# Gaps of 32 bytes between the pairs of transposed input tiles in SBUF

## The chip, the cores and the metric

The kernel runs on one core of a Trainium2 chip. The metric is the device time of one execution in microseconds (us). Two runs of the kernel before took 3258.87 and 3260.27 us, median 3259.57 us.

## The reference

Three transformer layers on one sequence of 512 tokens, width 1024, all in float32. Two layers have the form: half a gated feed-forward block (1024 to 2816 and back), a mixer of three branches (differential attention, chunked attention with a relative bias, retention) that are gated and summed, and another half feed-forward block. The third layer has dilated attention, a state-space scan and a gated linear recurrence side by side, then a feed-forward block and a final norm. Cut to what matters here, nearly all work is a matrix product of a normalised input with a weight matrix:

```
h = rms_norm(x, norm)
x = x + 0.5 * ((silu(h @ w_gate) * (h @ w_up)) @ w_down)
...
aq, ak, av, bq, bk, bv, cq, ck, cv, cg, gates = split(rms_norm(x, mix_norm) @ w_in)
```

## The kernel before, in words

The input is kept transposed: 8 tiles of 128 features by 512 tokens. A product of float32 precision is made of three single-pass matmuls in the type float32r. Each operand is split into a high part and a low part, and `mm3` (lines 406 to 411) issues high by high, low by high and high by low, into one accumulator in PSUM. This triple is the unit in which the prediction counts:

```
self.matmul(out, st[0], mv[0], start, False, c)
self.matmul(out, st[0], mv[1], False, False, c)
self.matmul(out, st[1], mv[0], False, stop, c)
```

`st` is the stationary operand, which is loaded into the array ahead of its matmul (the trace calls the load LDWEIGHTS, engine PEld), and `mv` the moving one, which streams through. In the trace a name out<-in,in gives the moving operand first.

The tiles in question are the 8 pairs `xgh0,xgl0` to `xgh7,xgl7`: high and low part of the scaled input, 128 partitions by 512 float32 each, 2048 bytes in a partition. `feed_norm` (line 591) allocates and fills them, one pair for each of the 8 blocks d of the features. They are used in two ways. In `fm_tile` (line 637) they are the moving operand and a weight block is stationary: 8 triples with d = 0 to 7, 512 columns each, make one output tile. In `tm_products` (line 644) the roles change: a slice of 128 tokens of `xgh` or `xgl` is stationary and the weights move, 384 or 512 columns. The weights are read from DRAM into the ring `raw` and split by ScalarE and VectorE into the rings `wh` and `wl` (lines 503 to 513), three buffers each, 4096 bytes in a partition; a unit of weights holds 8 blocks of 128 columns, 512 bytes each.

Tiles of one pool lie one behind the other in the order in which their names are first used, each rounded up to 32 bytes. Call the address of a tile within the partition, modulo 256, its place. In the kernel before, `wh` and `wl` start at 34048 and 46336, all 16 tiles `xgh`, `xgl` from 75008 on, 2048 bytes apart, and the feed-forward tiles `yh`, `yl` from 133888 and 156416 on: all these are at place 0, and so is every block of 512 bytes within them. A tile `warm` of 57 floats (line 452) ends the constants such that the rings behind it start at place 0.

One small unit of weights is different. `dt_unit` (line 1802) holds 8 blocks of only 8 columns each, 32 bytes, for a product with 8 outputs in the third layer. So its stationary operands lie at the places 0, 32, 64 and so on to 224, while the moving `xgh` and `xgl` are at 0. In the trace its matmuls are `b<-xgh,wh 128*8`.

The order of the program is made when it is built: a list scheduler with a cost for each operation resumes threads (`Net.ready`, `Net.wait`, class `Model`). Its numbers of buffers are those of the pools. The small tiles of the norm and the softmax (`rsy`, `rst`: 64 bytes, 7 buffers each; `nmax`, `sm`, `rc`: 32 bytes, 8 buffers each) lie in the pool behind the inputs.

## Time and profile before

| | |
|---|---|
| median of 2 runs | 3259.57 us |
| profiled execution, its own time | 3257.48 us |
| its span, first to last instruction | 3255.7 us |
| PE busy | 3232.1 us, 99% of the span, 15592 matmuls |
| PEld (weight loads) busy | 2713.4 us, 83% |
| DVE (VectorE) busy | 1870.9 us, 57% |
| ACT (ScalarE) busy | 1233.6 us, 38% |
| DMA, mean rate | 106 GB/s |
| mean granted TensorE clock | 0.996 of full speed |

1.8 us of the profiled execution's time lie around its span. A matmul is shown as busy from its start until its result is out, so consecutive matmuls overlap in the trace: one of 512 columns is shown as 389 ns long, and the next one starts well before its end. What a matmul takes from the engine is therefore read from start to start, called a step below, and not from its duration.

### The profile page before, as it was taken

What the parts mean: (1) busy time and instruction counts of PE and PEld (TensorE: products, weight loads), DVE (VectorE), ACT (ScalarE), POOL (GpSimd) and SP (SyncE); (2) the same over time, 40 slices, a digit from 0 to 9 for tenths busy, and PEclk for the clock granted to TensorE, in tenths of its full rate; (3) what the DMA queues carried; (4) which work ended last, traced back from release to release, by engine and by line L of the source; (5) the groups of instructions that cost most, each with busy time, mean ns of one, the idle gap of its engine ahead of it and who ended that gap; (6) DMA issues with size and microseconds to landing.
All of it is one profiled execution on the core that took longest, in us unless ns stands there. A gap on an engine that the chain in (4) does not pass through costs nothing.

```text
span 3255.7 us, 39837 instructions
## 1 busy us (share of the span) xinstructions
PE 3232.1 (99%) x15592; PEld 2713.4 (83%) x15592; DVE 1870.9 (57%) x3574; ACT 1233.6 (38%) x1996; POOL 111.6 (3%) x206
## 2 busy tenths in 40 slices
PE   9999999999999999999999999999999999999998
PEld 7888888878888888888888987888888788888888
DVE  5434578766754345434478766664344777564345
ACT  4223344653332223322344564333223346643223
POOL 0000000000100000000010000110000000000000
PEclk9999999999999999999999999999999999999999
DMA  4222443223423222222243322442223223222224
GB/s 143 97 97 97 130 118 112 88 84 110 171 92 102 95 94 97 97 97 97 94 138 115 112 90 76 139 149 97 97 97 110 103 72 106 81 88 97 97 97 143
DMA packets 106413, 343.51 MB, mean 106 GB/s; under 512 B 19680, under 2 KB 20864, under 8 KB 106224
## 3 DMA queue, kind: packets, MB, share of 16 engines
q1 hardware_dynamic: 83520, 289.04, 26.2%
q0 software_dynamic: 22704, 51.93, 4.6%
q8 instruction: 122, 2.00, 0.3%
q14 instruction: 67, 0.55, 0.1%
HBM read 319.88 MB, written 26.21 MB: 106 GB/s over the span
## 4 chain that ended last, share of the span: by engine, by line
PE 98%; DVE 1%; DMA 0%; ACT 0%; issue 0%; SPq 0%; DVEq 0%
PE acc L404 90%; PE b L404 7%; PE b L433 2%; DMA raw<-in_wst_dram 0%; DMA rowsA<-in_rows_dram 0%; DVE o L203 0%; DVE og L203 0%; ACT v L203 0%; DVE v L203 0%; DVE pT L203 0%; DVE y L203 0%; SPq L224 0%; DVE rst L203 0%; ACT y L203 0%; ACT pT L203 0%
## 5 line engine op out<-in xcount | busy, mean ns | idle before, releaser
L404 PE MATMUL acc<-xgh,wh 128*128 128x512 f32 x2432 | 959.4, 394 | 5.4 <-DVE v L203 3.9
L404 PE MATMUL acc<-xgl,wh 128*128 128x512 f32 x2432 | 949.6, 390 | 0.0
L404 PE MATMUL acc<-xgh,wl 128*128 128x512 f32 x2432 | 949.6, 390 | 0.0
L203 DVE TENSOR_TENSOR wl<-raw,wh 128x1024 fp32r<-128x1024 f32 (+3 forms) x563 | 669.1, 1189 | 459.9 <-ACT wh L203 457.6
L203 ACT CAST wh<-raw 128x1024 fp32r<-128x1024 f32 (+3 forms) x563 | 574.6, 1021 | 837.4 <-issue 432.8
L404 PEld LDWEIGHTS acc<-xgh,wh 128*128 128x128 f32 x2432 | 458.2, 188 | 104.4 <-DVE v L203 5.1
L404 PEld LDWEIGHTS acc<-xgh,wl 128*128 128x128 f32 x2432 | 457.9, 188 | 96.2
L404 PEld LDWEIGHTS acc<-xgl,wh 128*128 128x128 f32 x2432 | 458.2, 188 | 94.6 <-DVE xgl L203 1.5
L404 PE MATMUL acc<-yl,wh 128*128 128x512 f32 (+1 forms) x1032 | 378.2, 372 | 0.0
L404 PE MATMUL acc<-yh,wh 128*128 128x512 f32 (+1 forms) x968 | 358.1, 370 | 0.0
L404 PE MATMUL acc<-yh,wl 128*128 128x512 f32 (+1 forms) x968 | 357.9, 370 | 0.0
L404 PE MATMUL acc<-wh,xgh 128*128 128x384 f32 (+1 forms) x672 | 247.7, 369 | 0.0
L404 PE MATMUL acc<-wh,xgl 128*128 128x384 f32 (+1 forms) x672 | 236.0, 351 | 0.0
L404 PE MATMUL acc<-wl,xgh 128*128 128x384 f32 (+1 forms) x672 | 235.6, 351 | 0.0
L203 ACT ACTIVATE sg<-g 128x512 f32<-128x512 f32 x110 | 69.5, 632 | 431.8 <-DVE g L203 431.7
L404 PEld LDWEIGHTS acc<-yl,wh 128*128 128x128 f32 x1032 | 194.0, 188 | 33.3
L203 DVE TENSOR_TENSOR g<-acc,rbc 128x512 f32<-128x512 f32 x110 | 76.1, 691 | 234.8 <-PE acc L404 234.6
L404 PEld LDWEIGHTS acc<-yh,wh 128*128 128x128 f32 x968 | 182.4, 188 | 30.9
L404 PEld LDWEIGHTS acc<-yh,wl 128*128 128x128 f32 x968 | 182.4, 188 | 30.7
L203 DVE TENSOR_TENSOR u<-acc,rbc 128x512 f32<-128x512 f32 x110 | 76.0, 691 | 195.8 <-PE acc L404 195.8
L404 PEld LDWEIGHTS acc<-wh,xgh 128*128 128x128 f32 x672 | 127.7, 190 | 13.5 <-issue 5.3
L404 PEld LDWEIGHTS acc<-wl,xgh 128*128 128x128 f32 x672 | 127.7, 190 | 6.3
(276 smaller groups left out, 3337.3 us busy)
## 6 DMA issues: line engine op xcount, KB each, us to landing
raw<-in_wst_dram SPq DMA_DIRECT2D x496, 512.0 KB, 3.2
raw<-in_wst_dram SPq DMA_DIRECT2D x64, 384.0 KB, 3.6
gpark<-gl POOLq DMA_DIRECT2D x48, 256.0 KB, 4.2
mb<-gpark POOLq DMA_DIRECT2D x48, 256.0 KB, 3.6
xpark<-x POOLq DMA_DIRECT2D x24, 256.0 KB, 6.7
x<-xpark POOLq DMA_DIRECT2D x24, 256.0 KB, 4.9
relscr<-in_rel_dram POOLq DMA_DIRECT2D x8, 639.0 KB, 21.6
bias<-relscr POOLq DMA_DIRECT2D x16, 256.0 KB, 3.8
```

Source lines behind the costliest of these rows:

```text
L203: return f(*a, **k)
L404: self.nc.tensor.matmul(out, lhsT, rhs, start=start, stop=stop)
L433: self.nc.tensor.transpose(out, in_, ident)
```

## The change

Behind each of the first seven pairs, a tile of 8 floats (32 bytes) called `gap` is allocated and never used. It is allocated once in the program, when the pair is first filled. The pairs thereby move to 75008, 79136, 83264 and so on: the high and the low tile of pair d are both at place 32 d, from 0 to 224. The 224 bytes are taken from the pool behind: one buffer less for each of `rsy`, `rst`, `nmax`, `sm` and `rc` (2 times 64 and 3 times 32 bytes). So everything behind that pool stays where it was, the weights in front too. Inside the pool, the tiles `ss`, `sq` and `sq2` (sums of squares, and the operand `diag` of the matmuls that spread the norm) move from place 0 to 224, the tile `rbc` from 192 to 32, and the small tiles move as well.

In the built programs, every engine has the same instructions in the same order in both kernels, with the same waits: PE 15494, DVE 4366, ACT 2482, SP 1162, POOL 346, none of them different but for its addresses. Neither the scheduler's order nor any wait for a buffer changes, so no piece of the order is shown.

```diff
-        self.n = 0
+        self.n, self.spaced = 0, [False] * KD
...
-        y = self.sp.tile([P, 16], F32, tag="rsy", name=self.nm("rsy"), bufs=7)[:, :n]
-        t = self.sp.tile([P, 16], F32, tag="rst", name=self.nm("rst"), bufs=7)[:, :n]
+        y = self.sp.tile([P, 16], F32, tag="rsy", name=self.nm("rsy"), bufs=6)[:, :n]
+        t = self.sp.tile([P, 16], F32, tag="rst", name=self.nm("rst"), bufs=6)[:, :n]
...
             h = self.xp.tile([P, S], F32R, tag=f"xgh{d}", name=self.nm("xgh"))
             lo = self.xp.tile([P, S], F32R, tag=f"xgl{d}", name=self.nm("xgl"))
+            if d < KD - 1 and not self.spaced[d]:
+                self.xp.tile([P, 8], F32, tag=f"gap{d}", name=self.nm("gap"))
+                self.spaced[d] = True
...
-        return (p,) + tuple(self.sp.tile([P, 2], F32, tag=t, name=self.nm(t), bufs=8) for t in ("nmax", "sm", "rc"))
+        return (p,) + tuple(self.sp.tile([P, 2], F32, tag=t, name=self.nm(t), bufs=7) for t in ("nmax", "sm", "rc"))
```

## Rows read from the trace of the kernel before

**Rows 1.** The page: busy us (share of span); the chain's shares by engine, by line.

```profile
PE 3232.1 (99%) x15592; PEld 2713.4 (83%) x15592; DVE 1870.9 (57%) x3574; ACT 1233.6 (38%) x1996; POOL 111.6 (3%) x206
...
PE 98%; DVE 1%; DMA 0%; ACT 0%; issue 0%; SPq 0%; DVEq 0%
PE acc L404 90%; PE b L404 7%; PE b L433 2%; DMA raw<-in_wst_dram 0%; DMA rowsA<-in_rows_dram 0%; DVE o L203 0%; DVE og L203 0%; ACT v L203 0%; DVE v L203 0%; DVE pT L203 0%; DVE y L203 0%; SPq L224 0%; DVE rst L203 0%; ACT y L203 0%; ACT pT L203 0%
```

**Rows 2.** Span and mean granted TensorE clock of the core.

```profile
core 0: 3255.7 us, clock 0.996
```

**Rows 3.** Groups by shape, PE: out<-moving,stationary, xcount | busy us, mean ns | idle.

```profile
L404 PE MATMUL acc<-xgh,wh 128*128 128x512 f32 x2432 | 959.4, 394 | 5.4 <-DVE v L203 3.9 <-ACT xgh L203 1.5
...
L404 PE MATMUL acc<-wh,xgh 128*128 128x384 f32 x512 | 180.3, 352 | 0.0
...
L404 PE MATMUL acc<-wh,xgh 128*128 128x512 f32 x160 | 67.5, 422 | 0.0
...
L404 PE MATMUL b<-diag,ones 128*128 128x512 f32 x52 | 20.5, 400 | 0.2 <-DVE diag L203 0.2
...
L404 PE MATMUL b<-xgh,wh 128*8 128x512 f32 x8 | 3.2, 395 | 0.0
```

**Rows 4.** The chain in order of time: start us, length us, engine and line, xcount.

```profile
931.81 354.28 PE acc L404 x1563
...
2199.47 350.20 PE acc L404 x1545
...
3218.33 25.57 PE acc L404 x213
```

**Rows 5.** Timeline of PE in a feed-forward stage: start us, duration us, operation.

```profile
1300.26 0.39 PE L404 MATMUL acc<-xgh,wh 128*128 128x512 f32 x1
1300.48 0.39 PE L404 MATMUL acc<-xgl,wh 128*128 128x512 f32 x1
1300.71 0.39 PE L404 MATMUL acc<-xgh,wl 128*128 128x512 f32 x1
1300.94 0.39 PE L404 MATMUL acc<-xgh,wh 128*128 128x512 f32 x1
```

**Rows 6.** Timeline of PE, the product of the 8-column weights (dt_unit).

```profile
2549.51 0.39 PE L404 MATMUL b<-xgh,wh 128*8 128x512 f32 x1
2549.74 0.39 PE L404 MATMUL b<-xgl,wh 128*8 128x512 f32 x1
2549.96 0.39 PE L404 MATMUL b<-xgh,wl 128*8 128x512 f32 x1
2550.19 0.40 PE L404 MATMUL b<-xgh,wh 128*8 128x512 f32 x1
2550.42 0.40 PE L404 MATMUL b<-xgl,wh 128*8 128x512 f32 x1
2550.66 0.39 PE L404 MATMUL b<-xgh,wl 128*8 128x512 f32 x1
2550.88 0.40 PE L404 MATMUL b<-xgh,wh 128*8 128x512 f32 x1
...
2553.43 0.39 PE L404 MATMUL b<-xgh,wl 128*8 128x512 f32 x1
2553.66 0.28 PE L404 MATMUL b<-ones,sq 128*128 128x1 f32 x2
```

**Rows 7.** Timeline of PE behind a few narrow attention matmuls.

```profile
435.46 0.44 PE L404 MATMUL acc<-xgh,wh 128*128 128x512 f32 x1
435.74 0.40 PE L404 MATMUL acc<-xgl,wh 128*128 128x512 f32 x1
435.98 0.39 PE L404 MATMUL acc<-xgh,wl 128*128 128x512 f32 x1
436.21 0.39 PE L404 MATMUL acc<-xgh,wh 128*128 128x512 f32 x1
436.43 0.39 PE L404 MATMUL acc<-xgl,wh 128*128 128x512 f32 x1
```

## The prediction, made before the changed kernel ran

> **What bounds the kernel now.** I read the page first: PE is busy for 99% of the span, and the chain of work that ended last is PE for 98%, nearly all of it the matmul line of the big products [rows 1]. [...] No other engine is near the bound (DVE 57%, ACT 38%). Only what changes the step of a matmul, from its start to the next one's start, can change the time.

> Then the chain in order of time gives that step. In the feed-forward stages it holds runs of matmuls of 512 columns without any other engine in them: 354.28 us for 1563 and 350.20 us for 1545, 226.67 ns each in both; a run of 256 columns near the end has 25.57 us for 213, 120.0 ns [rows 4]. From 256 to 512 columns the step grows by 106.6 ns, which is 256 columns at 2.4 GHz. So a step is the columns at 2.4 GHz plus about 13.3 ns, whatever the width: 226.67 - 213.33, and 120.0 - 106.7. [...] The timeline of such a stage shows the even beat of 0.22 to 0.23 us; a triple, from one `xgh,wh` to the next, takes 0.68 us [rows 5].

> Last I looked for places where this step is not 226.67 ns though operands, shape and clock are alike. There are two. Behind narrow attention matmuls the steps are 0.28, 0.24, 0.23 us, then 0.22 again [rows 7]; no engine is waited for there. So the step depends on when in some beat a matmul starts, and the undisturbed stages have settled on a start that fits. And in the product of 8-column weights, where the stationary operand's place runs through 0, 32, ..., 224, the first triple (place 0) takes 2550.19 - 2549.51 = 0.68 us, the five after it 2553.66 - 2550.19 = 3.47 us, 0.694 us each, in steps of 0.23, 0.24 and 0.22 [rows 6]. The first is the normal triple, and each triple at another place is 14 ns longer: in two of its three steps the start comes some 7 ns late. All of them are alike, at 32 as at 160. This is the one spot of the trace where operands of such matmuls are not both at place 0.

> **The change part by part.** *Instructions, order and waits.* None is added, removed or moved, on any engine or queue, so there is nothing to price. The smaller numbers of buffers could make a writer wait for a reader, but each instruction waits for the same semaphore values as before, so they cost 0.

> *Tiles that ScalarE and VectorE use.* `ss`, `sq`, `rbc` and the small tiles move to other places. VectorE has 43% of the span free and ScalarE 62% [rows 1], and the feed-forward runs hold none of their work in the chain [rows 4], so even some per cent on these operations stay hidden. Without that cover, 1% of DVE's 1870.9 us would be 19 us. I take 0. The 52 `diag` matmuls [rows 3] get a moving operand at 224; at 14 ns each that would be 0.7 us, which I leave out.

> *The input pairs.* Triples with `xgh` and `xgl`: 2432 with them moving, 512 and 160 with them stationary [rows 3], together 3104 (without the 8 of the 8-column weights). Seven of eight have d from 1 to 7 and leave place 0 while the other operand stays there: 2716 triples, 8148 matmuls. The trace of before has no moving operand of this type away from place 0, so the price of a triple needs bounds. Low end: 0, if only the distance between the low bits within the 8-column blocks mattered there. A gain isn't excluded either, since the 13.3 ns are still there to lose. High end from the nearest row: 14 ns for a triple, as with the 8-column weights [rows 6], 2716 x 0.014 = 38.0 us. I take the middle, 7 ns for a triple, 19.0 us. The reason: in [rows 6] it was the stationary operand that was off, which holds here for only 672 of the 3104 triples; for the others what is sure is that the place changes once for each triple, from one pair to the next, and a start that no longer fits is late by one such 7 ns unit, as it is in single steps of both [rows 6] and [rows 7]. In a triple both tiles share a place, so its other two steps can settle.

> Sum against the profiled execution: 3257.48 + 19.0 = 3276.5 us. Its time is 2.1 us below the median of the two runs, so about 3278 us for a median.

> [...]

> **The rivals.** *No change.* The 14 ns of [rows 6] would belong to blocks of 8 columns, which lie closer together than all others, or to their short load, and not to places in general. For it: the settled step is the same for `xg` against `wh` as at the end for `yh` tiles, whose distance to the weights is another multiple of 256. Against it: all five disturbed triples are alike though their places differ, while the one at place 0 with the same short load is normal. Time 3257 to 3262 us.

> *Faster: a lucky seam or a step without its excess.* Moving and stationary reads that both begin at place 0 at the same moment might be what costs the 13.3 ns, and a moving operand that starts elsewhere would lose part of it. If one 7 ns unit goes in each triple, the gain is 19 us: 3238 to 3241 us. If it goes in each matmul, it is 8148 x 6.7 ns = 54.6 us: about 3205 us. [...] For it: the excess is exact, 13.3 ns at 256 columns as at 512 [rows 4], as if something were waited for. Against it: in [rows 6] the places of the two operands do differ, the load is tiny, and no step is below 0.22 us. It decides from the point at which a start away from place 0 lets the next stream begin a unit earlier. [...]

> *Much slower: the beat is lost.* If the changing place keeps the matmuls from ever settling, every step is like the late ones of [rows 7], 0.233 us or more: 8148 x 7 ns = 57 us, and up to 75 us at 9 ns. Time 3315 to 3335 us. For it: the place changes every 0.68 us, and in [rows 7] it took three steps to settle. Against it: in [rows 6] the place also changes with each triple, and every third step is normal again.

> *The change doesn't do what it says.* The gaps would have to be missing in the built program; the allocation puts the pairs 4128 bytes apart, so I give this no chance of its own.

> **How the numbers follow.** Slower by half a unit to two units per triple, 3266 to 3300 us: 0.45, and my forecast, 3278 us. No change, 3255 to 3266 us: 0.25. Faster within 2%: 0.14. Faster by more than 2%: 0.06. The beat lost, 3300 us and more: 0.10, of which 0.06 is within reach of 2% or beyond. The range from 3228 to 3315 us takes in the forecast's own case, no change, the gain of one unit per triple and the start of the lost beat; it leaves out the larger gains and the far end of the losses, together about 0.2. A change of 2%, about what a measurement of this kernel can tell from no change, is 65 us: below 3194 or above 3325 us. Faster 0.06, slower 0.06, within 2% 0.88.

> **What would show it.** If the forecast is right, the long runs in the chain of waits still have 1563 and 1545 matmuls without another engine in between, but the mean step in the part where `xgh` moves is 229 ns instead of 226.67, and the part where `yh` and `yl` move keeps 226.67. The timeline shows one late step in a triple for d from 1 to 7, and none at d = 0. With no change both parts keep 226.67 ns. With a gain the `xgh` part falls below 226 ns. With the lost beat, two or three steps of each triple are at 233 ns or more. The durations on DVE and ACT stay as they are; if their busy sums move by more than 1%, places matter to them too, and my 0 for them has to be looked at. I am wrong if the time leaves the range while the `xgh` steps stay at 226.67 ns: then the cause lies outside the matmuls' operands.

## The result

The changed kernel took 3296.88 us (median of 2 runs, 3296.24 and 3297.52) against 3259.57 us, 37 us more. The quotient of these two medians is 1.0114; the ratio on record is 1.0129, 95% interval 1.0104 to 1.0153. The changed kernel is slower, clear of noise, by less than 2%. The prediction had 3278 us, with a range of 3228 to 3315 us. The direction and the place of the effect were right, the size was half of what was measured, and the reason given for that size did not hold.

### The profile page after: what moved, and what is told of

Read it like the earlier page. It is cut to its first block, busy times and chain, and to the rows that moved or that the text cites. A ratio compares the mean times of both kernels' runs of the same rounds, so it can differ in the third digit from the quotient of the medians.

```text
span 3294.5 us, 39837 instructions
## 1 busy us (share of the span) xinstructions
PE 3269.6 (99%) x15592; PEld 2712.1 (82%) x15592; DVE 1871.6 (57%) x3574; ACT 1232.6 (37%) x1996; POOL 111.5 (3%) x206
## 4 chain that ended last, share of the span: by engine, by line
PE 98%; DVE 1%; DMA 0%; ACT 0%; issue 0%; SPq 0%; DVEq 0%
PE acc L404 90%; PE b L404 7%; PE b L433 2%; DMA x<-in_xT_dram 0%; DMA rowsA<-in_rows_dram 0%; DVE o L203 0%; DVE og L203 0%; ACT v L203 0%; DVE v L203 0%; DVE pT L203 0%; DVE y L203 0%; DVE rst L203 0%; ACT y L203 0%; ACT pT L203 0%; DVE mb L203 0%
## 5 line engine op out<-in xcount | busy, mean ns | idle before, releaser
L404 PE MATMUL acc<-xgh,wh 128*128 128x512 f32 x2432 | 971.8, 400 | 6.6 <-DVE v L203 3.9
L404 PE MATMUL acc<-xgh,wl 128*128 128x512 f32 x2432 | 962.4, 396 | 0.0
```

The costliest lines, as they stand in the source:

```text
L404: self.nc.tensor.matmul(out, lhsT, rhs, start=start, stop=stop)
```

## The profile after

First the page and the chain in order of time of the changed kernel (columns as in [rows 4]). The lines answer to [rows 1] and [rows 4].

```profile
PE 3269.6 (99%) x15592; PEld 2712.1 (82%) x15592; DVE 1871.6 (57%) x3574; ACT 1232.6 (37%) x1996; POOL 111.5 (3%) x206
...
PE 98%; DVE 1%; DMA 0%; ACT 0%; issue 0%; SPq 0%; DVEq 0%
```

```profile
941.82 360.36 PE acc L404 x1563
...
2224.28 356.19 PE acc L404 x1545
...
3256.60 25.57 PE acc L404 x213
```

PE grew by 37.5 us, nearly the whole of it. The other engines kept their busy times within 1.3 us (PEld -1.3, DVE +0.7, ACT -1.0), so the tiles that moved for VectorE and ScalarE show no cost. The granted clock is 0.996 in both. The two long runs still have 1563 and 1545 matmuls without another engine between them, but are 6.1 and 6.0 us longer; all five of this kind together went from 1712.6 to 1742.1 us, 29.5 of the 38.8 us by which the span grew. The last run, of 256 columns with `yh` and `yl` moving and no `xgh` in it, kept its 25.57 us to the digit.

Counted from the starts, 1035 of the 1563 matmuls of the first long run have the inputs moving, and 528 the feed-forward tiles. The step of the 1035 went from 226.67 to 232.46 ns, 5.8 ns each, 17.4 ns for a triple; the 528 have 226.66 before and 226.81 now. The groups say which use of the inputs pays (PE, by shape, columns as in [rows 3]):

```profile
L404 PE MATMUL acc<-xgh,wh 128*128 128x512 f32 x2432 | 971.8, 400 | 6.6 <-DVE v L203 3.9 <-ACT xgh L203 2.7
L404 PE MATMUL acc<-xgh,wl 128*128 128x512 f32 x2432 | 962.4, 396 | 0.0
L404 PE MATMUL acc<-xgl,wh 128*128 128x512 f32 x2432 | 957.5, 394 | 0.3 <-DVE xgl L203 0.3
...
L404 PE MATMUL acc<-wh,xgh 128*128 128x384 f32 x512 | 181.4, 354 | 0.0
```

With the inputs moving, the three groups of 2432 grew by 12.4, 12.8 and 7.9 us (the first was 959.4 in [rows 3], the other two 949.6 each). With the inputs stationary, the group of 512 grew by 1.1 us (180.3 in [rows 3]). Since shown durations overlap, the sums from start to start are the better measure: 36.1 us more for the 7296 matmuls with the inputs moving, 1.4 us for the 2016 with them stationary. In the second use the new places are nearly free here, 0.7 ns a matmul against 5.0.

Last the timeline of PE over one output tile. Shown are the starts of its eight triples (d = 0 to 7) and of the next tile; the two other matmuls of each are left out.

```profile
1399.62 0.40 PE L404 MATMUL acc<-xgh,wh 128*128 128x512 f32 x1
...
1400.31 0.40 PE L404 MATMUL acc<-xgh,wh 128*128 128x512 f32 x1
...
1401.00 0.40 PE L404 MATMUL acc<-xgh,wh 128*128 128x512 f32 x1
...
1401.70 0.40 PE L404 MATMUL acc<-xgh,wh 128*128 128x512 f32 x1
...
1402.40 0.39 PE L404 MATMUL acc<-xgh,wh 128*128 128x512 f32 x1
...
1403.10 0.40 PE L404 MATMUL acc<-xgh,wh 128*128 128x512 f32 x1
...
1403.81 0.39 PE L404 MATMUL acc<-xgh,wh 128*128 128x512 f32 x1
...
1404.50 0.40 PE L404 MATMUL acc<-xgh,wh 128*128 128x512 f32 x1
...
1405.19 0.40 PE L404 MATMUL acc<-xgh,wh 128*128 128x512 f32 x1
```

The triples take 0.69, 0.69, 0.70, 0.70, 0.70, 0.71, 0.69 and 0.69 us, 5.57 us in all, where each took 0.68 in [rows 5]. The first, whose pair is still at place 0, is longer too. Over the 22 output tiles of one stretch of the first long run the triples with d = 0 take 693 ns in the mean and all eight 697 ns, against 680 before.

## The experiments

Three theories stood against each other. **Distance:** what costs is that the moving and the stationary operand lie at different places. **Seam:** what costs is the change of place from pair to pair, which was the reason for the size I had forecast. **Absolute:** a moving operand away from place 0 costs by itself. A fourth, the other tiles that moved, had to be ruled out first. Below, distance means the stationary operand's place minus the moving one's, modulo 256. The kernel before, run beside the first group on the same chip, took 3256.66 us, beside the second 3254.9 us.

### One gap behind all pairs

```diff
-            if d < KD - 1 and not self.spaced[d]:
-                self.xp.tile([P, 8], F32, tag=f"gap{d}", name=self.nm("gap"))
-                self.spaced[d] = True
+            if not self.spaced[d] and {7: 56}.get(d):
+                self.xp.tile([P, {7: 56}[d]], F32, tag=f"gap{d}", name=self.nm("gap"))
+            self.spaced[d] = True
```

> The 224 bytes lie in one piece behind the last pair: all pairs are at place 0 as before, while everything else (fewer small buffers, ss, sq, sq2 and diag at place 224, rbc at 32) is as in the changed kernel. If the inputs' places are the cause (distance, seam or absolute place): 3257 to 3262 us. If the other moved tiles are: 3290 to 3300 us.

3260.56 us, ratio 1.0007, interval 0.9996 to 1.0018. Fewer buffers and the other moved tiles cost nothing clear of noise: 3.9 us by the medians, inside the interval. The places of the pairs are the cause.

### All pairs at place 32

```diff
+            if not self.spaced[d] and {0: 8}.get(d):
+                self.xp.tile([P, {0: 8}[d]], F32, tag=f"gb{d}", name=self.nm("gap"))
             h = self.xp.tile([P, S], F32R, tag=f"xgh{d}", name=self.nm("xgh"))
...
-            if d < KD - 1 and not self.spaced[d]:
-                self.xp.tile([P, 8], F32, tag=f"gap{d}", name=self.nm("gap"))
-                self.spaced[d] = True
+            if not self.spaced[d] and {7: 48}.get(d):
+                self.xp.tile([P, {7: 48}[d]], F32, tag=f"gap{d}", name=self.nm("gap"))
+            self.spaced[d] = True
```

> All eight pairs at place 32, weights at 0; the place does not change from pair to pair, 192 bytes behind the last pair. Distance theory (moving and stationary operand at different places cost): slower, at least the 14 ns for a triple of the 8-column product, for 3104 triples 43 us, 3300 us. Seam theory (the change of place from pair to pair costs): 3257 to 3262 us. Absolute theory (a moving operand away from 0 costs): slower, 3290 to 3305 us, but then e3 as well.

3303.33 us, ratio 1.0142, interval 1.0124 to 1.0160. The seam theory falls as the account of the cost: without any change of place from pair to pair the kernel is 46.7 us slower, more than the changed one. (That a change of place costs something as well is shown below, at line 46 of the run of matmuls alone.) The two long runs of [rows 4] in its chain:

```profile
940.12 361.25 PE acc L404 x1563
...
2227.25 357.06 PE acc L404 x1545
```

6.97 us more in the first, over its 1035 matmuls with the inputs moving, are 6.7 ns each, 20 ns for a triple.

### Everything shifted by 32

```diff
-        warm = c.tile([P, 1 + 56], F32, name="warm")[:, 0:1]
+        warm = c.tile([P, 1 + 64], F32, name="warm")[:, 0:1]
```

> The kernel before with 32 bytes more in front of everything: weights, inputs and feed-forward tiles all at place 32, their distances as before. Distance theory and seam theory: 3257 to 3262 us. Absolute theory: every product is off, so more than the changed kernel's 3297 us, about 3330 us.

3253.95 us, ratio 0.9994, interval 0.9982 to 1.0005. The absolute theory falls, the distance theory holds: with all operands at 32, the long run takes what it took in [rows 4]:

```profile
931.31 354.28 PE acc L404 x1563
```

### The places alone

```python
    for r in ROWS:
        for s in ROWS:
            for k in range(N):
                nc.tensor.matmul(acc, st[s], mv[r], start=k == 0, stop=k == N - 1)
    for t in range(8):
        for r in ROWS:
            for k in range(3):
                nc.tensor.matmul(seq, st["A"], mv[r], start=(r == "A" and k == 0), stop=(r == "H" and k == 2))
...
```

`ROWS` is A to H and `N` is 24. The second loop, line 42, is the changed kernel's sequence; it stands twice more, with `st[r], mv[r]` (line 46) and with `st[r], mv["A"]` (line 50).

> Only matmuls, none of the reference is computed: each of 8 moving tiles (places 0 to 224, A to H) against each of 8 stationary tiles (same places), 24 in a row; then the triples of the changed kernel in sequence against a stationary tile at 0, against one at the moving one's place, and moving at 0 against stationary tiles at 0 to 224. Distance theory: A-A, B-B to H-H 226.7 ns a step, all others 230 ns or more. Absolute theory: all of row A 226.7 ns, the other rows slower alike. Seam theory: all 64 at 226.7 ns, since no place changes within 24, and only the sequences are slower, by the 5.9 ns a matmul of the changed kernel.

This ran once, at a mean granted clock of 0.996; from 4.02 to 495.81 us its chain holds nothing but matmuls. The timeline gives for each group of 24 its start, length and operands (moving, stationary). One group's start to the next one's is 24 steps, of which the first few still settle.

```profile
33.58 5.77 PE L38 MATMUL acc<-mvA,stF 128*128 128x512 f32 x24
39.19 5.67 PE L38 MATMUL acc<-mvA,stG 128*128 128x512 f32 x24
44.69 5.76 PE L38 MATMUL acc<-mvA,stH 128*128 128x512 f32 x24
50.28 5.77 PE L38 MATMUL acc<-mvB,stA 128*128 128x512 f32 x24
55.89 5.64 PE L38 MATMUL acc<-mvB,stB 128*128 128x512 f32 x24
61.37 5.75 PE L38 MATMUL acc<-mvB,stC 128*128 128x512 f32 x24
66.96 5.76 PE L38 MATMUL acc<-mvB,stD 128*128 128x512 f32 x24
```

Matched, B against B, 24 steps take 5.48 us; A against G, distance 192, 5.50 us; the others 5.59 to 5.61 us. The mean of the settled steps (the 7th to the 23rd of each group) by distance, worked out from the starts; along each diagonal of the 8 by 8 groups all values agree within 1 ns, but for the group at the very start:

```
distance    0     32     64     96    128    160    192    224
ns      226.6  233.4  233.5  234.2  233.6  233.5  228.7  233.2
```

So in a row of equal matmuls of this shape the distance decides, and nothing else of the two places that was tried. The price is not proportional to it: about 7 ns at six distances, 2.1 ns at 192, nothing at 0.

The changed kernel's sequence repeats its triples one for one (A to H are d = 0 to 7, line 42), and the next lines show the sequence in which both operands move on together (line 46):

```profile
401.19 0.86 PE L42 MATMUL seq<-mvA,stA 128*128 128x512 f32 x3
401.88 0.86 PE L42 MATMUL seq<-mvB,stA 128*128 128x512 f32 x3
402.57 0.86 PE L42 MATMUL seq<-mvC,stA 128*128 128x512 f32 x3
403.27 0.86 PE L42 MATMUL seq<-mvD,stA 128*128 128x512 f32 x3
403.97 0.86 PE L42 MATMUL seq<-mvE,stA 128*128 128x512 f32 x3
404.67 0.87 PE L42 MATMUL seq<-mvF,stA 128*128 128x512 f32 x3
405.38 0.86 PE L42 MATMUL seq<-mvG,stA 128*128 128x512 f32 x3
406.07 0.86 PE L42 MATMUL seq<-mvH,stA 128*128 128x512 f32 x3
406.76 0.86 PE L46 MATMUL seq<-mvA,stA 128*128 128x512 f32 x3
407.46 0.86 PE L46 MATMUL seq<-mvB,stB 128*128 128x512 f32 x3
```

From start to start the triples of line 42 take 0.69, 0.69, 0.70, 0.70, 0.70, 0.71, 0.69 and 0.69 us, the same eight numbers as in the changed kernel. Eight moving tiles, one stationary tile and a chain of nothing but matmuls (362.30 to 406.93 us for line 42) reproduce it. And line 46, once settled, takes 694 ns for a triple (231.4 ns a step), as line 50 does in the mean, though every matmul of line 46 has its two operands at one place. So in this sequence a change of place from triple to triple costs some 14 ns by itself, against 680 ns without one (three matched steps of 226.6 ns). A candidate for the cause is the load for the next triple, which is already at the next place. Where a group ends, the timeline shows when that load runs:

```profile
61.13 0.40 PE L38 MATMUL acc<-mvB,stB 128*128 128x512 f32 x1
61.14 0.65 PEld L38 LDWEIGHTS acc<-mvB,stC 128*128 128x128 f32 x3
61.37 0.62 PE L38 MATMUL acc<-mvB,stC 128*128 128x512 f32 x2
```

This is the last matmul of B against B. Its own operands match, its step is 0.24 us (235 ns, after steps of 226 to 227), and what runs beside it is the load of C. At the ends of all seven matched groups B to H it is the same. Conversely, six of the eight groups at distance 224 end with a step of 226 or 227 ns, where the next load matches the stream; such a group has no step under 230 ns otherwise. By these two readings it would be the place of the load for the next matmul that counts, rather than that of the operand in use. It is not shown: in line 46 the step beside the load of the next place is 231 ns, and the longest, 235 ns, is the one before it; and in [rows 6] the third step of the first triple, which runs beside the load at place 32, is still 226 ns.

### Loads and sizes

```python
run("same" + r, [(mv["A"], st["A"]), (mv[r], st[r])] * 18)
run("swap" + r, [(mv["A"], st[r]), (mv[r], st["A"])] * 18)
run(name + r, [(mv["A"], st[r][:, 0:w])] * 24, w=w)            # w = 8, 32, 64
run(name + r, [(mv["A"][:, 0:n], st[r])] * 24, n=n)            # n = 256, 384
run("finem" + r, [(wide[:, k:k + S], narrow[:, 0:P])] * 24)    # k = 0 to 7 floats
run("full" + r, [(raw[0], full[r])] * 12)                      # plain float32
```

> Only matmuls, none of the reference is computed. Operands A to H at places 0 to 224 as in e4. 'same' alternates (moving A, stationary A) with (moving r, stationary r); 'swap' alternates (A, r) with (r, A). If the operand in use counts: same 226.7 ns a step, swap 233 ns. If the operand that is loaded for the next matmul while this one streams counts: same 233 ns (r = B, C, E), swap 226.7 ns. Then moving A against stationary tiles of 8, 32 and 64 columns: if the load's length sets the price, 8 columns cost less than 233 ns. 256 and 384 columns moving: the same 6.8 ns on 120.0 and 173.3 ns if the price belongs to the load, in proportion to the columns if it belongs to the stream. Shifts of 4 to 28 bytes of the moving or the stationary operand: 226.7 ns if 32 bytes are the grain, otherwise another step, perhaps a shorter one than 226.7 ns. Plain float32 operands (two passes at half the rate): the same step at all places.

The chain has one line for each group: start, length, name and count. A length has about 0.4 us of fixed start and end in it, so groups of equal count and width are compared. The steps below are worked out from the starts. This ran once, too.

```profile
17.84 8.65 PE sameB L46 x36
...
26.53 8.59 PE swapB L46 x36
...
99.27 5.63 PE eightA L46 x24
...
110.67 5.74 PE eightC L46 x24
...
238.27 3.15 PE nhalfA L46 x24
...
260.48 3.08 PE nhalfH L46 x24
263.60 4.45 PE nmostA L46 x24
...
277.09 4.45 PE nmostD L46 x24
...
286.11 4.51 PE nmostF L46 x24
...
329.10 6.03 PE finemF L46 x24
...
393.83 10.58 PE fullA L46 x24
404.46 10.58 PE fullB L46 x24
```

The alternation of places does not tell load from use: `same` and `swap` are alike, at 228 to 232 ns a step, so neither expectation came true and the question stays open. The other parts say more:

- A load of 8 columns, 32 bytes, costs 5 ns a step at C (5.74 against 5.63 us), where one of 128 columns costs 7. The other distances have 4 to 5 ns, 192 among them, and B has 2. So the price is not in proportion to the load. Loads of 32 or 64 columns did not settle at 226.7 ns even matched (231.5 and 229.7 ns).
- With 384 columns moving, six of the eight groups, A to D, G and H, stay at 173.2 to 173.5 ns; E has 175.6 and F 176.6; with 256 columns every distance is within 0.2 ns of the matched 120.0 ns or below it, down to 116.6 ns at 224. The price of 7 ns was seen at 512 columns alone.
- Shifts by 4 to 28 bytes give 226.6 to 240 ns (F is 20 bytes), none below 226.6. So 32 bytes are not the grain, and none of the shifts tried gives a shorter step at this width.
- Plain float32, which shows 24 records for 12 matmuls, two passes of 512 columns at 429 ns each (1.9 times the 226.6 ns of a single-pass matmul), has the same 10.58 us for a group at all five places tried (A, B, C, E and G).

### All pairs at place 64, all pairs at place 128

The edit is that of place 32, with 16 floats in front and 40 behind for place 64, and 32 in front and 24 behind for place 128.

> All pairs at place 64, weights at 0. In e4 moving 64 against stationary 0 has 228.9 ns a step, 2.1 ns over the matched one, where moving 32 has 6.8 ns, and e2 (all at 32) was 46.7 us slower. If the distance alone sets the price: 46.7 x 2.1 / 6.8 = 14 us slower, 3271 us. If any place but the weights' own costs the same: 3303 us.

> All pairs at place 128, weights at 0. In e4 moving 128 against stationary 0 has 233.6 ns a step, 6.9 ns over the matched one. Distance theory: as e2, about 47 us slower, 3304 us. If the price grew with the distance in bytes: four times e2's, 3440 us. If only the low bits below 128 counted: 3257 us.

Place 64: 3273.86 us, ratio 1.0057, interval 1.0041 to 1.0073: 19 us by the medians, 13 to 24 us by the interval. Place 128: 3300.42 us, ratio 1.0136, interval 1.0119 to 1.0153, 45.5 us by the medians. Both follow the table of distances (192 and 128), and neither the bytes nor the seam theory. The first long run at 64 has 2.42 us more than [rows 4] over its 1035 matmuls with the inputs moving, 2.3 ns each, where the table has 2.1:

```profile
935.77 356.70 PE acc L404 x1563
```

## Why the prediction was off, point by point

- **The bound and the place of the effect** were right: PE's step alone, in [rows 4] and [rows 5], and of the 38.8 us of the span 36.1 lie, from start to start, in the matmuls with the inputs moving and 1.4 in those with them stationary.
- **Order, waits, other engines, the other moved tiles at 0**: right, shown by the run with one gap (3260.56 against 3256.66 us).
- **The evidence of [rows 6]** was read rightly as one of place. But the distance is not the whole rule there. In the changed kernel the same eight-column matmuls are matched in themselves, and of the six triples in a row (from 2580.30 us) those at places 0, 64 and 128 take 0.68 us, those at 32, 96 and 160 still 0.70 us. Why is open.
- **The step that failed** is the price of a triple, "I take the middle, 7 ns for a triple". The runs put 17.4 ns in its place in the long runs, and 15 ns over all 2432 triples with the inputs moving. Its reason, that only the change of place costs and the two other steps "can settle", is the seam theory, which the run at 32 refutes: a distance costs 6.7 ns in each step, with no change of place at all. The change of place was undersized as well: by itself it costs 14 ns a triple (line 46), and the sign that the forecast named, one late step for d from 1 to 7 and none at d = 0, did not appear.
- **The high end** of the sum, 38.0 us, meets the measured 37 us, but by luck: its errors cancel. In the long runs a triple with the inputs moving costs 17.4 ns and not 14. The triples with d = 0, priced at 0, cost 13 ns; triple A of line 42, with both operands at place 0, takes 694 ns as well, and why was not shown. The 672 triples with the inputs stationary, priced like the others, cost almost nothing, 1.4 us in all; 512 of them have 384 columns moving, where the run of loads and sizes has 173.2 to 173.5 ns at six of eight places. And outside the long runs about a third of the steps with the inputs moving were off 226.67 ns already: the five long runs lose 17.4 ns in each of their 1672 triples, 29.1 us, the other 760 triples 9 ns each, 7.0 us.
- **The rivals.** No change fell, and so did every gain: no settled step of a run here at 512 columns is below 226.6 ns. The lost beat, from 0.233 us a step on, came near: the changed kernel's long runs have 232.5 ns where the inputs move. My argument against it was that every third step of [rows 6] is normal again; that holds for a moving operand of one place, and not once it moves.
- **Two numbers in the working.** Up to 9 ns on 8148 matmuls are 73 us, not 75. And 2% is not about what a measurement of this kernel can tell: the interval here reaches 0.25% to either side, so 1.3% is clear.
- **What the working took for granted.** That a step depends on when in some beat a matmul starts was an estimate of mine from the four steps of [rows 7]; no run isolates the start. "2.4 GHz" is a rate worked out from [rows 4], 256 columns in 106.67 ns or 2.40 a ns; the trace gives the clock only as a share, 0.996. A third width agrees with the step worked out from it: 384 columns give 160.0 + 13.3 = 173.3 ns, against 173.2 to 173.5 ns at six of the eight places.

## What to carry to other kernels

Where single-pass float32 matmuls of 512 moving and 128 stationary columns bind, as here with PE at 99% of the span, let the moving operand and the weights start at the same place modulo 256 (226.6 ns a step, against 233.2 to 234.2 ns at six of the seven other distances), and let that place not change from one triple to the next (694 instead of 680 ns in line 46). Which place it is made no difference: 3253.95 us with all at 32, 3256.66 us with all at 0. Eight floats in front of one of the two operands' tiles were enough to lose 1.4% (all pairs at place 32). A step of one matmul read from starts, in stretches with nothing else on the chain, shows such a loss (226.67 and 232.46 ns); the busy share of PE is 99% in both kernels and does not.
